# A hybrid attention block on one core: a host-transposed input normalised in place, sixteen gate steps at the front, and a tail two Strassen groups shorter

## The chip, the cores and the metric

The kernel runs on one core of a Trainium2 chip. The metric is the device time of one execution in microseconds; the kernel before takes 1904.11 (median of three runs, 1903.36 to 1904.30). A core has TensorE (PE in the profile), which multiplies matrices out of SBUF into PSUM; VectorE (DVE), ScalarE (ACT) and GpSimd (POOL), which work elementwise; and SyncE (SP), whose queue issues most of the DMA transfers here. Each engine works through its own list of instructions in order.

## The reference

One layer of a block over 2048 tokens of 1024 channels: an RMS norm, one wide projection for two attention mixers, SiLU gates on both mixers' outputs, and a sigmoid-weighted merge added to the residual. Cut to what matters here:

```python
h = rms_norm(x, norm_gain[layer])            # x * rsqrt(mean(x*x) + eps) * gain
proj = h @ w_in[layer]
qa, ka, va, qb, kb, vb, ga, gb, mg = jnp.split(proj, split_idx, axis=-1)
...                                          # banded attention A, dilated attention B
ya = ya.reshape(bsz, S, A_WIDTH) * jax.nn.silu(ga)     # ga: 512 channels
yb = yb.reshape(bsz, S, B_WIDTH) * jax.nn.silu(gb)     # gb: 512 channels
br_a = ya @ w_branch_a[layer]
br_b = yb @ w_branch_b[layer]
gates = jax.nn.sigmoid(mg...)
merged = gates[:, :, 0] * br_a + gates[:, :, 1] * br_b
x = x + merged @ w_out[layer]
```

The gates ga and gb are 1024 channels, so eight chunks of 128.

## The kernel before

**Numbers.** float32 products are made of float16 parts: each operand is split in a high and a low half, and a product is the sum of three matmuls (high by high, high by low, low by high) over eight chunks of 128 channels. One gate step is therefore 24 matmuls of 128x512. The normalised input lies in SBUF as XH and XL, channels on the partitions, tokens along the row.

**Stages.** (1) The input stage loads x, normalises it, makes XH and XL, and already computes two of the eight gate chunks. (2) The main stage projects and attends, unit by unit (unit A (0,0), A (1,0), then the dilated units), up to about 1230 us. In it, when a chunk of a mixer's output is ready for 512 tokens, a `YPart` transposes it on TensorE; for gate chunks 0 and 1 it fetches the stored gate, multiplies on VectorE (L966) and takes the maximum (L973), for the others ScalarE only copies it out (L964). (3) The tail computes the merge gates and the other six silu gate chunks with one level of Strassen's scheme: 19 groups in the order of the table `SEQ`, each 7 products of 12 matmuls (L1607). Entries 8, 9 and 10 of the table are the silu weights, two groups each, 1 to 7 the merge gates. Beside them the tail prepares the branch and output weights in 16 pieces, due between group 4 and group 17 (`K_AT`). (4) The branch products, the merge and the output projection follow.

**The input stage.** SP loads the gain (broadcast to all partitions, 512 KB), 16 tiles of x (128 tokens by 1024 channels, 512 KB each), two gate weights (512 KB) and four parts of the first unit's weights (384 KB). For each tile ScalarE squares and sums (L443), VectorE makes the inverse root with ScalarE's logarithm and exponential, and multiplies the tile by it and by the gain (L464); TensorE transposes it in eight pieces of 128x128 float32 (L484); ScalarE rounds the high half out of PSUM (L487) and VectorE subtracts for the low half (L491). As soon as 512 tokens are ready, two gate steps follow (L354), each with a tanh on ScalarE (L364), a gate product on VectorE (L371) and a store by SP (L377): four quarters by two chunks, eight steps.

**What sets the order.** In the input stage and in the tail a small planner does. Each step is entered with its engine, a cost in microseconds (`X_US` in the input stage), what it needs, and a rank; the planner plays the steps through these costs and writes them to the engines' lists in the order that comes out. On the chip only that order and the real dependences count. SP's loads stand in the order of `X_LD`.

## Time and profile before

| | |
|---|---|
| runs | 1903.36, 1904.11, 1904.30 us |
| profiled execution, span | 1902.2 us (from the first to the last instruction; the runs lie 1.2 to 2.1 above it) |
| granted TensorE clock | 1.000 |
| busy: TensorE, VectorE, ScalarE, GpSimd | 1871.2, 1499.1, 1249.0, 581.6 us |
| input stage ends (first main-stage matmul in the chain) | 80.90 us |
| Strassen groups, last before the standard steps | 1247.7 to 1580.5 us |

In the page, a group of instructions reads: line, engine, operation, output and inputs with their shapes and a count, then busy time, mean nanoseconds of one, the engine's idle time before it, and what ended that. A row of windows holds the stretch, then each engine's busy time with its number of instructions, then the granted clock, the DMA engines' mean share and GB/s. A row of the chain holds start, duration, engine and line of the piece that everything after waited for.

### The profile page before, as it was taken

What the parts mean: (1) busy time and instruction counts of PE and PEld (TensorE: products, weight loads), DVE (VectorE), ACT (ScalarE), POOL (GpSimd) and SP (SyncE); (2) the same over time, 40 slices, a digit from 0 to 9 for tenths busy, and PEclk for the clock granted to TensorE, in tenths of its full rate; (3) what the DMA queues carried; (4) which work ended last, traced back from release to release, by engine and by line L of the source; (5) the groups of instructions that cost most, each with busy time, mean ns of one, the idle gap of its engine ahead of it and who ended that gap; (6) DMA issues with size and microseconds to landing.
All of it is one profiled execution on the core that took longest, in us unless ns stands there. A gap on an engine that the chain in (4) does not pass through costs nothing.

```text
span 1902.2 us, 51103 instructions
## 1 busy us (share of the span) xinstructions
PE 1871.2 (98%) x19254; PEld 1439.5 (76%) x19254; DVE 1499.1 (79%) x3837; ACT 1249.0 (66%) x3015; POOL 581.6 (31%) x1363
## 2 busy tenths in 40 slices
...
GB/s 257 83 103 203 168 194 137 199 168 157 171 148 180 140 155 202 146 166 176 142 176 145 146 153 134 172 300 184 202 201 187 191 154 274 295 162 121 143 149 76
DMA packets 638983, 326.21 MB, mean 171 GB/s; under 512 B 458768, under 2 KB 589712, under 8 KB 636304
## 3 DMA queue, kind: packets, MB, share of 16 engines
...
q10 hardware_dynamic: 144, 0.26, 0.0%
...
## 4 chain that ended last, share of the span: by engine, by line
PE 91%; DMA 5%; DVE 1%; ACT 1%; issue 1%; SPq 0%; POOL 0%; DVEq 0%; POOLq 0%
PE pj L693 43%; PE fps L1607 18%; PE fps L1927 8%; PE fps L2012 7%; PE s L846 5%; PE pv L895 4%; PE pj L354 2%; DMA pt<-p 2%; PE pj L306 2%; DMA kq<-spl 1%; PE fps L306 1%; PE pt L959 1%; DMA bigl<-sd 1%; DMA graw<-in_w_gate_dram 0%; PE s L484 0%
## 5 line engine op out<-in xcount | busy, mean ns | idle before, releaser
L693 PE MATMUL pj<-wl,XH 128*128 128x128 f16 (+2 forms) x2816 | 715.2, 268 | 0.0
L693 PE MATMUL pj<-wh,XL 128*128 128x128 f16 (+2 forms) x2816 | 711.6, 269 | 0.0
L693 PE MATMUL pj<-wh,XH 128*128 128x128 f16 (+2 forms) x2816 | 708.6, 268 | 0.0
L693 PEld LDWEIGHTS <-XH 128*128 128x128 f16 x5632 | 574.9, 112 | 54.1
L693 PEld LDWEIGHTS <-XL 128*128 128x128 f16 x2816 | 315.8, 112 | 23.8
L861 DVE CUSTOM_DVE_ANT_0 pr<-s,b,ubuf 128x256 f32<-128x256 f32 (+3 forms) x512 | 218.7, 464 | 39.1 <-PE s L846 36.1
L878 DVE SCALAR_TENSOR_TENSOR p<-pr,p 128x512 f16<-128x512 f32 (+2 forms) x256 | 195.9, 765 | 49.7 <-ACT p L874 48.4
L760 POOL TENSOR_TENSOR rw<-rw,g 128x128 f32<-128x128 f32 (+1 forms) x224 | 149.2, 686 | 198.8 <-DVE rw L753 177.8
L1937 POOL TENSOR_TENSOR g<-g,t 128x512 f32<-128x512 f32 x32 | 48.4, 1514 | 522.1 <-DVE t L1859 521.6
L1607 PEld LDWEIGHTS <-wh 128*128 128x128 f16 x1064 | 104.2, 99 | 123.4 <-issue 0.3
L711 ACT ACTIVATE rw<-pj 128x256 f32<-128x256 f32 (+1 forms) x224 | 87.4, 390 | 135.8 <-PE pj L693 135.3
L775 POOL COPY spl<-spl 128x256 f16<-128x256 f16 (+1 forms) x224 | 97.4, 464 | 241.8 <-DVE spl L770 241.8
L874 ACT ACTIVATE p<-pr 128x512 f16<-128x512 f32 (+2 forms) x256 | 157.6, 616 | 10.7 <-DMA pt<-p 6.3
L846 PE MATMUL s<-kq 128*128 128x128 f16 (+1 forms) x1984 | 151.1, 217 | 2.7 <-DMA kq<-spl 1.6
L1927 PE MATMUL fps<-y,bigh 128*128 128x128 f16 x1792 | 153.4, 219 | 0.0
L1927 PE MATMUL fps<-y,bigl 128*128 128x128 f16 x896 | 151.7, 219 | 0.0
L2012 PE MATMUL fps<-WO,mf 128*128 128x512 f16 x660 | 147.5, 379 | 0.0
L846 PEld LDWEIGHTS <-kq 128*128 128x128 f16 x2016 | 131.0, 98 | 18.9 <-issue 3.5
L1927 PEld LDWEIGHTS <-bigh 128*128 128x128 f16 x1792 | 139.0, 98 | 7.3
L895 PE MATMUL pv<-vt,pt 128*128 128x65 f16 (+1 forms) x2784 | 131.6, 193 | 5.7 <-DMA pt<-p 5.7
L895 PEld LDWEIGHTS <-pt 128*128 128x128 f16 x3024 | 119.5, 97 | 21.0 <-DMA pt<-p 8.1
L766 ACT ACTIVATE spl<-rw 128x512 f16<-128x512 f32 (+1 forms) x112 | 72.0, 643 | 79.3 <-POOL vt L722 67.4
...
## 6 DMA issues: line engine op xcount, KB each, us to landing
...
g<-mgd SPq DMA_DIRECT2D x64, 256.0 KB, 5.1
wraw<-in_w_mrg_dram SPq DMA_DIRECT2D x45, 256.0 KB, 4.3
mgd<-t SPq DMA_DIRECT2D x43, 256.0 KB, 2.8
zd<-z SPq DMA_DIRECT2D x128, 66.0 KB, 2.0
...
xt<-in_x_dram SPq DMA_DIRECT2D x16, 512.0 KB, 8.0
ytd<-yo SPq DMA_DIRECT2D x32, 256.0 KB, 3.3
```

Source lines behind the costliest of these rows:

```text
L693: out.append(lambda lhs=lhs, rhs=rhs, ch=ch, a=a, b=b, k=k: T.matmul(ps[:, a:b], lhsT=lhs[:, ch, :], rhs=rhs[:, ch, a:b], start=(k == 0), ...
L711: A.activation(self.rw[:, n * i:n * i + n], self.ps[i][:, :n], AF.Copy)
L760: G.tensor_tensor(q[:, i, :un.nq, :], q[:, i, :un.nq, :], g, OP.mult)
L775: G.tensor_copy(sp[:, i, nh:, :, :], sp[:, i, nq:nh, ::-1, :])
L846: T.matmul(self.sv[j][:, o:o + k1 - k0], lhsT=q[:, h, :], rhs=kt[:, un.nq + kh + v * un.nk, k0:k1], start=(v == 0), stop=(v == 1))
L861: V.tensor_tensor_reduce(out=self.pv[:, j, self.p0:self.p0 + W], in0=self.sv[j], in1=un.bias[:, self.h0 + j, self.b0:self.b0 + W], scale=I ...
L874: A.activation(self.sp[:, :128 * n], self.pr, AF.Copy, scale=PSC)
L878: V.scalar_tensor_tensor(self.sp[:, 128 * n:], self.pr, PSC, self.sp[:, :128 * n], OP.mult, OP.subtract)
L895: T.matmul(self.po[:, j, :w], lhsT=p[:, n * j + s, :], rhs=un.v[key][:, vh, c0:c0 + w], start=(k == 0 and s == 0), stop=(k == 2 and s == n ...
L1607: T.matmul(b[k][:], lhsT=w[:, i, ch, :], rhs=xform(PROD[i][0], lo, ch, q), start=(i < 3 and n == 0), stop=(n == 11), skip_group_check=True)
L1927: out.append(lambda p=p, c=c, wl=wl, yl=yl, n=n: T.matmul(ps[:, 128 * p:128 * p + 128], lhsT=w[wl][:, i, c, p, :], rhs=y[:, yl, c, :], sta ...
L2012: out.append(lambda p=p, ml=ml, wl=wl, k=k: T.matmul(ps[:], lhsT=m[:, ml, p, :], rhs=WO[:, i, wl, p, :], start=(fresh and k == 0), stop=(k ...
```

## The change

**Input.** The host hands the kernel a second copy of x, transposed to eight chunks of 128 channels by 2048 tokens. It is loaded in five parts (256, 256, 512, 512 and 512 tokens) and normalised where it lies; there are no transposes. Parts 0 and 1 get their row sums from TensorE: a product of each 128 tokens with themselves (L525), whose diagonal VectorE sums (L512), and after the inverse root a diagonal matrix by ones (L565), which lays the factors along the row. Parts 2 to 4 still load tiles 4 to 15 of x as it was, for ScalarE's squares (L506); the inverse root is ten small operations on VectorE (L548 to L552), ScalarE's queue writes the four columns of 128 factors to memory (L572), and SP fetches them back as a row R, broadcast to all partitions (L576). The multiplication by R is VectorE's (L581) or GpSimd's (L583), by the table `X_DVE`; ScalarE makes the high half with the gain as its scale (L587), VectorE the low half from two operands in SBUF (L591).

**Gates.** Four chunks instead of two (`NSI`), so 16 steps (matmuls L383, tanh L393, product L400, store L406), the first quarter's in two halves of 256 tokens. The weights' norms are taken by TensorE (L329); chunks 2 and 3 are scaled and split on GpSimd (L373, L366). `YPart` takes the fetching and multiplying way for chunks 2 and 3 too, which come with unit A (1,0). Fourteen small matmuls stand ahead of everything on TensorE (L517).

**Tail.** `SEQ` loses the two groups of entry 10, so 17 groups, and the pieces' last due group is 15. `SX` and `VSC` are powers of two that scale numbers.

SP's queue, in which loads stand in the order in which they are issued (`xt` is the tile of x, `graw` a gate weight, `wraw` a unit's weight, `gtd` a stored gate). Before:

```order
L469 DMA gb<-in_gain_dram 128x1024
L423 DMA xt<-in_x_dram 128x1024 x4
L316 DMA graw<-in_w_gate_dram 128x1024
L423 DMA xt<-in_x_dram 128x1024 x2
L426 DMA qg<-in_qkg_dram 128x256
L427 DMA snk<-in_sink_dram 128x8
L428 DMA bmt<-in_b_merge_dram 128x16
L316 DMA graw<-in_w_gate_dram 128x1024
L423 DMA xt<-in_x_dram 128x1024 x8
L180 DMA wraw<-in_w_units_dram 128x768 x4
L423 DMA xt<-in_x_dram 128x1024 x2
```

Now, from the loads of tiles 4 to 7 on (ahead of them stand, in this order, the gain, two `xq`, two `graw`, two `xq`, the three small loads and two `graw`; `xq` is the transposed x, `rd` the factors in memory):

```order
L456 DMA xt<-in_x_dram 128x1024 x4
L464 DMA xq<-in_xt_dram 128x2x512 x4
L456 DMA xt<-in_x_dram 128x1024 x2
L183 DMA wraw<-in_w_units_dram 128x768 x4
L456 DMA xt<-in_x_dram 128x1024 x5
L576 DMA R<-rd 128x512
L464 DMA xq<-in_xt_dram 128x2x512 x4
L456 DMA xt<-in_x_dram 128x1024
L406 DMA gtd_88<-yo 128x512
L406 DMA gtd_89<-yo 128x512
L464 DMA xq<-in_xt_dram 128x2x512 x4
L576 DMA R<-rd 128x512
```

The first fetch of R stands behind 23 loads of 512 KB and four of 384 KB, where before all 16 tiles, the gain, both gate weights and the four `wraw` were 19 and four.

VectorE around the third quarter's tokens, before (a product with the factor, then low halves out of PSUM, `s`):

```order
L464 SCALAR_TENSOR_TENSOR xt<-xt,xr,gb 128x1024
L491 TENSOR_TENSOR XL<-s,XH 128x4x128 x3
L464 SCALAR_TENSOR_TENSOR xt<-xt,xr,gb 128x1024
L447 TENSOR_SCALAR xss<-xss 128x4
L491 TENSOR_TENSOR XL<-s,XH 128x4x128 x2
L371 SCALAR_TENSOR_TENSOR yo<-yo,pj 128x512
L491 TENSOR_TENSOR XL<-s,XH 128x4x128 x3
L371 SCALAR_TENSOR_TENSOR yo<-yo,pj 128x512
```

Now, the multiplications and low halves of parts 3 and 4:

```order
L581 TENSOR_TENSOR xq<-xq,R 128x512 x5
L400 SCALAR_TENSOR_TENSOR yo<-yo,pj 128x512
L591 SCALAR_TENSOR_TENSOR XL<-xq,gs,XH 128x512 x6
L400 SCALAR_TENSOR_TENSOR yo<-yo,pj 128x512
L591 SCALAR_TENSOR_TENSOR XL<-xq,gs,XH 128x512 x2
L581 TENSOR_TENSOR xq<-xq,R 128x512 x3
L400 SCALAR_TENSOR_TENSOR yo<-yo,pj 128x512
L591 SCALAR_TENSOR_TENSOR XL<-xq,gs,XH 128x512 x6
```

Every operation of VectorE between the gate products now has both operands in SBUF, where half of them had one in PSUM.

GpSimd, which had one copy in the stage before, now does this up to its first main-stage copy (L594):

```order
L583 TENSOR_TENSOR xq<-xq,R 128x256 x4
L373 TENSOR_SCALAR graw<-graw,gps_358 128x1024 x2
L366 TENSOR_TENSOR gl<-graw,gh 128x1024 x2
L583 TENSOR_TENSOR xq<-xq,R 128x256 x2
L583 TENSOR_TENSOR xq<-xq,R 128x512 x12
```

The twelve last rows' worth of products are those of parts 2, 3 and 4 that VectorE does not have.

The diff, cut to its core:

```diff
-VSC = 2.0 ** -16
-SX = 2.0 ** 8
+VSC = 2.0 ** -13
+SX = 2.0 ** 9
...
-SEQ = ((1, 0), (1, 1), (8, 0), (8, 1), (2, 0), (2, 1), (9, 0), (9, 1), (3, 0), (3, 1), (10, 0), (10, 1), (4, 0), (4, 1),
+SEQ = ((1, 0), (1, 1), (8, 0), (8, 1), (2, 0), (2, 1), (9, 0), (9, 1), (3, 0), (3, 1), (4, 0), (4, 1),
        (5, 0), (5, 1), (6, 0), (6, 1), (7, 0))
+NSI = 4
 G_T0, G_LD, G_SQ = 5.0, 6.0, 2.0
 W_RAW, L_LAST = 14.0, 0.4
-STD, W_EARLY, G_TH, G_SI, G_CP, K_AT = 5.2, 24.0, 2.0, 4.0, 1.0, (4, 17)
+STD, W_EARLY, G_TH, G_SI, G_CP, K_AT = 5.2, 24.0, 2.0, 4.0, 1.0, (4, 15)
 Y_S = 4.0
 Y_1 = (.2, .9, 1.6), (13.0, 14.0, 1.6)
 WO_AT = 2.0, 5.5
 M_AT = {0: (1.0, (5.0, 6.6, 8.2, 9.8, 11.4, 13.0, 14.6)), 1: (1.0, (6.5, 8.7, 10.9, 13.1, 15.3, 17.5, 19.7)),
         7: (.7, (3.5, 5.4, 7.3, 9.2, 11.1, 13.5, 26.4))}
-X_LD = ("g", 0, 1, 2, 3, "w0", 4, 5, "w1", 6, 7, 8, 9, 10, 11, 12, 13, "u")
-X_RK = (-35, 21, 20, -9)
-X_TR = 0.6
-X_NR = (-34, -92, 28)
-X_XR = (7, -126, 40, 10)
-X_GR = (29, 49)
-X_TWO = (0, 1, 2, 2)
-X_GF = (6.6, 15.2)
-X_TH = (45, 46, 85, 86, 125, 126, 165, 166)
+X_LD = ("g", "a0", "w0", "w1", "a1", "w2", "w3", 4, 5, 6, 7, "t2", 8, 9, 10, 11, "t3", 12, 13, 14, 15, "u", "t4")
+X_PART = ((0, 256), (256, 256), (512, 512), (1024, 512), (1536, 512))
...
+X_DVE = {0: ((), (0, 2, 4, 6)), 1: ((), (0, 1, 3, 4, 6, 7)), 2: ((), (0, 3, 5, 6)), 3: ((), (0, 3, 4, 5, 6)), 4: ((), (0, 2, 4))}
...
+XR_BUFS = 6
+XT_BUFS = 2
+X_WARM = 14
...
+    def g_gram(c, ch):
+        if ch == 0:
+            grams["g", c] = s_p.tile([128, 512], F32, name="s") if c % 2 else pj_p.tile([128, 512], F32, name="pj")
+        v = gw[c][0][:, ch, :]
+        T.matmul(grams["g", c][:, 0:128], lhsT=v, rhs=v, start=(ch == 0), stop=(ch == NCH - 1))
...
+    def g_lo(c, pool):
         gh, gl, ih, raw, s = gw[c]
-        V.scalar_tensor_tensor(gl[:], raw, s[:], gh[:], OP.mult, OP.subtract)
-        done.add(("g", c))
+        if pool:
+            G.tensor_tensor(gl[:], raw, gh[:], OP.subtract)
+        else:
+            V.scalar_tensor_tensor(gl[:], raw, s, gh[:], OP.mult, OP.subtract)
+    def g_scale(c):
+        gh, gl, ih, raw, s = gw[c]
+        gw[c] = (gh, gl, ih, raw, 1.0)
+        G.tensor_scalar(raw, raw, s, None, OP.mult)
...
-        ps = pj_p.tile([128, 512], F32, name="pj")
-        ts = slice(512 * q, 512 * q + 512)
-        out = []
-        for w, xx in ((gh, XH), (gh, XL), (gl, XH)):
-            for ch in range(NCH):
-                i = len(out)
-                out.append(lambda w=w, xx=xx, ch=ch, i=i: T.matmul(
-                    ps[:], lhsT=w[:, ch, :], rhs=xx[:, ch, ts], start=(i == 0), stop=(i == 23)))
-        return out, gate_steps(ps, c, q, ih, None)
+        ps = pv_p.tile([128, 512], F32, name="pv") if q == 0 and c > 1 else pj_p.tile([128, 512], F32, name="pj")
+        def mm(k, a, b):
+            w, xx = ((gh, XH), (gl, XH), (gh, XL))[k // NCH]
+            ch = k % NCH
+            T.matmul(ps[:, a:b], lhsT=w[:, ch, :], rhs=xx[:, ch, 512 * q + a:512 * q + b], start=(k == 0), stop=(k == 23))
+        return mm, gate_steps(ps, c, q, ih, None)
...
+    def t_load(p, i, n):
+        t0, m = X_PART[p]
+        if i == 0:
+            if p != 1:
+                xq[0] = sp0.tile([128, NCH, 512], F32, name="xq", bufs=XT_BUFS)
+            xtt[p] = xq[0][:, :, t0 % 512:t0 % 512 + m]
+        nc.sync.dma_start(out=xtt[p][:, i:i + n, :], in_=xt[i:i + n, :, t0:t0 + m].rearrange("c p t -> p c t"))
...
-    def x_scale(t):
-        i = t - groups[t][0]
-        V.scalar_tensor_tensor(xts[t][:], xts[t][:], xss[groups[t]][:, i:i + 1], gb[:], OP.mult, OP.mult)
...
-    def x_turn(t, h):
-        xps[t, h] = ps = s_p.tile([128, 4, 128], F32, name="s")
-        for c in range(4):
-            cc = 4 * h + c
-            T.transpose(ps[:, c, :], xts[t][:, 128 * cc:128 * cc + 128], idf[:])
-    def x_hi(t, h):
-        A.activation(XH[:, 4 * h:4 * h + 4, 128 * t:128 * t + 128], xps[t, h][:], AF.Copy)
-    def x_lo(t, h):
-        ts = slice(128 * t, 128 * t + 128)
-        V.tensor_tensor(XL[:, 4 * h:4 * h + 4, ts], xps[t, h][:], XH[:, 4 * h:4 * h + 4, ts], OP.subtract)
...
+    def x_warm(i):
+        if i == 0:
+            grams["w"] = pt_p.tile([128, 512], F32, name="pt")
+        T.matmul(grams["w"][:, 0:128], lhsT=ones[:], rhs=ones[:], start=True, stop=True)
+    def x_gram(p, c):
+        if c == 0:
+            for i in range(2):
+                grams[2 * p + i] = s_p.tile([128, 512], F32, name="s") if p == 0 else pv_p.tile([128, 512], F32, name="pv")
+        for i in range(2):
+            v = xtt[p][:, c, 128 * i:128 * i + 128]
+            T.matmul(grams[2 * p + i][:, 0:128], lhsT=v, rhs=v, start=(c == 0), stop=(c == NCH - 1))
+    def x_trace(t):
+        p, i = t // 2, t % 2
+        if i == 0:
+            rs_[p] = sp0.tile([128, 4], F32, name="xss", bufs=4)
+        trace(grams[t], rs_[p][:, i:i + 1])
...
+    def x_rsqrt(p):
+        ss = rs_[p][:]
+        y = sp0.tile([128, 4], F32, name="xy", bufs=4)
+        h = sp0.tile([128, 4], F32, name="xh", bufs=4)
+        V.tensor_scalar(y[:].bitcast(I32), ss.bitcast(I32), -0.5, float(0x5F3759DF), OP.mult, OP.add)
+        for k in range(3):
+            V.tensor_tensor(h[:], y[:], y[:], OP.mult)
+            V.scalar_tensor_tensor(h[:], h[:], -0.5, ss, OP.mult, OP.mult)
+            V.scalar_tensor_tensor(y[:] if k < 2 else ss, h[:], 1.5, y[:], OP.add, OP.mult)
+    dgs, rps = {}, {}
+    def x_diag(t):
+        p, i = t // 2, t % 2
+        dgs[t] = sp0.tile([128, 128], F32, name="dg", bufs=2)
+        V.tensor_scalar(dgs[t][:], idf[:], rs_[p][:, i:i + 1], None, OP.mult)
+    def x_row(t):
+        p, i = t // 2, t % 2
+        if i == 0:
+            rps[p] = s_p.tile([128, 512], F32, name="s")
+        T.matmul(rps[p][:, 128 * i:128 * i + 128], lhsT=ones[:], rhs=dgs[t][:], start=True, stop=True)
+    def x_rows(p):
+        Rt[p] = sp0.tile([128, 512], F32, name="R", bufs=2)
+        A.activation(Rt[p][:, 0:256], rps[p][:, 0:256], AF.Copy)
+    def x_spread(p):
+        nc.scalar.dma_start(out=rd[p - 2].rearrange("i t -> t i"), in_=rs_[p][:])
+    def x_fetch(p):
+        Rt[p] = sp0.tile([128, 512], F32, name="R", bufs=2)
+        nc.sync.dma_start(out=Rt[p][:], in_=rd[p - 2].rearrange("i t -> (i t)").unsqueeze(0).broadcast_to([128, 512]))
+    def x_mul(p, c, dve):
+        v = xtt[p][:, c, :]
+        if dve:
+            V.tensor_tensor(v, v, rps[p][:, 0:256] if p < 2 else Rt[p][:], OP.mult)
+        else:
+            G.tensor_tensor(v, v, Rt[p][:, :X_PART[p][1]], OP.mult)
+    def x_hi(p, c):
+        t0, m = X_PART[p]
+        A.activation(XH[:, c, t0:t0 + m], xtt[p][:, c, :], AF.Copy, scale=gs[:, c:c + 1])
+    def x_lo(p, c):
+        t0, m = X_PART[p]
+        V.scalar_tensor_tensor(XL[:, c, t0:t0 + m], xtt[p][:, c, :], gs[:, c:c + 1], XH[:, c, t0:t0 + m], OP.mult, OP.subtract)
...
+                elif p > 2:
+                    free = [("lo", b, c) for b in ((0, 1) if p == 3 else (2,)) for c in range(NCH)]
+            else:
+                f, args = x_load, (k,)
+                if k >= XR_BUFS + 4:
+                    free = [("sq", k - XR_BUFS)]
...
+            pool = c in X_GLP
+            if pool:
+                od.add(("gc", c), "G", us_["gc"], [("gp", a)], 0, g_scale, c)
+            od.add(("gh", c), "A", us_["gh"], [("gc", c) if pool else ("gp", a)], 0, g_hi, c)
+            od.add(("gl", c), *(("G", us_["pl"], [("gh", c)]) if pool else ("V", us_["gl"], [("gh", c)])), 0, g_lo, c, pool, first=X_GL1 if c == 1 else 0.0)
...
+    gates = [(q, c) for q in range(4) for c in range(NSI)]
+    runs = [(i, p) for p in range(2) for i in range(NSI)] + [(i, gates[i][0] + 1) for i in range(NSI, 4 * NSI)]
...
-            if self.chunk > 1:
+            if self.chunk >= NSI:
...
-        c = 2 + 2 * (dc - 8) + n
+        c = NSI + 2 * (dc - 8) + n
...
-        for c in range(8)] + [_rows(w[:, 5632 + 256 * c:5888 + 256 * c]) for c in range(3)])
+        for c in range(8)] + [_rows(w[:, 5376 + 256 * c:5632 + 256 * c]) for c in range(NSI // 2, 4)])
...
-    return [x[0], w_units, w_gate, w_mrg, wo, w_bra, w_brk, norm_gain, qkg, sink_a, bias_a, bias_b, bm]
-_INS = ["x", "w_units", "w_gate", "w_mrg", "w_out", "w_bra", "w_brk", "gain", "qkg", "sink", "bias_a", "bias_b", "b_merge"]
+    return [x[0], x[0].T.reshape(NCH, 128, S), w_units, w_gate, w_mrg, wo, w_bra, w_brk, norm_gain[0].reshape(NCH, 128).T, qkg, sink_a, bias_a, bias_b, bm]
```

326 lines of the change are left out of this document (209 added, 117 removed).

## The prediction

> **What bounds the kernel now.** I read the page's head first, then the core's windows, the chain of waits, and the groups. The head says which engine to watch:
>
> ```profile
> span 1902.2 us, 51103 instructions
> PE 1871.2 (98%) x19254; PEld 1439.5 (76%) x19254; DVE 1499.1 (79%) x3837; ACT 1249.0 (66%) x3015; POOL 581.6 (31%) x1363
> ```
>
> TensorE (PE) is busy for all but 31 us of the span. The stretches of ten microseconds show where most of those 31 us are; PE's busy time is the second number of a row.
>
> ```profile
> 0.00:10.00 10.00, 0.00 (x0) 0.00 (x0) 4.01 (x14) 4.72 (x8) 0.84 (x7) 1.00 0.80 299
> 10.00:20.00 10.00, 6.28 (x28) 5.77 (x28) 8.94 (x26) 9.20 (x22) 0.00 (x0) 1.00 0.98 376
> 20.00:30.00 10.00, 9.11 (x33) 4.55 (x34) 8.83 (x20) 9.90 (x19) 0.00 (x0) 1.00 1.03 418
> ...
> 60.00:70.00 10.00, 10.00 (x60) 6.03 (x60) 9.83 (x18) 7.46 (x11) 1.12 (x3) 1.00 0.09 33
> ...
> sum 90.00, PE 72.10 PEld 43.16 DVE 64.92 ACT 61.21 POOL 1.96; mean PE 8.01 PEld 4.80 DVE 7.21 ACT 6.80 POOL 0.22
> ```
>
> PE is idle for 17.9 of the first 90 us, 14.6 of them before 30 us, while DMA runs at 418 GB/s. So two prices count: loads until the first gate step, and PE time everywhere else. The chain gives both:
>
> ```profile
> 2.12 6.62 DMA xt<-in_x_dram
> 8.76 8.28 DMA graw<-in_w_gate_dram
> ...
> 22.83 7.79 PE pj L354 x27
> ...
> 68.16 0.87 PE s L484 x8
> 69.03 11.87 PE pj L354 x55
> 80.90 14.14 PE pj L693 x87
> ```
>
> The first gate matmul starts at 22.83, and the stage hands over to the main stage at 80.90. One warm gate matmul (L354) costs 11.87/55 = 0.2158 us, a step of 24 of them 5.18. One of the removed transposes (L484) costs 0.87/8 = 0.109.
>
> **The change, part by part.**
>
> *The tail.* Two of the 19 Strassen groups go, each 7 products of 4 chunks by 3 split terms = 84 matmuls (L1607).
>
> ```profile
> 1525.98 0.12 PE fps L191 x2
> 1526.10 54.41 PE fps L1607 x252
> 1400.00:1450.00 50.00, 50.00 (x234) 22.79 (x233) 38.91 (x81) 38.86 (x77) 0.00 (x0) 1.00 0.73 218
> 1500.00:1550.00 50.00, 50.00 (x235) 22.86 (x234) 35.50 (x76) 41.55 (x79) 0.00 (x0) 1.00 0.60 185
> ```
>
> One matmul is 54.41/252 = 0.2159, so two groups are 168 x 0.2159 = 36.3, plus one norm sum of 0.12 for the weight preparation that goes with them: **-36.4 us**. PE is busy for the whole of both windows, so nothing there now hides behind something else. The 16 weight pieces of the later table are now spread over 11 groups instead of 13. ACT's fullest window is 41.55 of 50; if nothing but the number of groups changed, that would be 41.55 x 13/11 = 49.1, just inside 50. The dropped gates' own work leaves too, so I charge nothing, and keep this as a rival.
>
> *The input stage, by PE's work.* 16 steps instead of 8 are 8 x 5.18 = +41.4; 128 transposes go, 128 x 0.109 = -14.0. That alone would move 80.9 to 108.3, if the waits stayed. The warm-up matmuls and the gram matmuls lie in PE's early idle time. But the waits are now others, so I also build the end from the loads.
>
> *When the second quarter can begin.* Parts 2 to 4 cannot be multiplied before R, the row of 512 token factors, has been fetched, and the first fetch stands on SP behind 23 loads of 512 KB, four of 384 KB and the small ones. SP's queue of before shows the pace, as each issue waits for an earlier load:
>
> ```profile
> 5.01 0.33 SPq L426 DMA_DIRECT2D qg<-in_qkg_dram  x1
> 6.27 0.33 SPq L427 DMA_DIRECT2D snk<-in_sink_dram  x1
> 7.52 0.33 SPq L428 DMA_DIRECT2D bmt<-in_b_merge_dram  x1
> 8.76 0.33 SPq L316 DMA_DIRECT2D graw<-in_w_gate_dram  x1
> ```
>
> So the first 512 KB land at 5.0 and then one each 1.25. The second graw, ninth of its size, should have landed at 5.0 + 8 x 1.25 = 15.0; by the chain it did at 8.76 + 8.28 = 17.04. The three small loads therefore cost 2.0. The 23rd lands at 5.0 + 22 x 1.25 + 2.0 = 34.5; four weight loads of three quarters size add 3.75, and R's 256 KB 0.6: **38.9**. R is read from a small write of r that comes from ACT's queue, and no write of such small elements is in this trace; the nearest rows are a store and the input loads:
>
> ```profile
> xt<-in_x_dram SPq DMA_DIRECT2D x16, 512.0 KB, 8.0
> ...
> gtd<-yo SPq DMA_DIRECT2D x1, 256.0 KB, 2.3
> ```
>
> Between 2.3 and 8.0 us from issue to landing, then, the long one for a write in the thick of the loads. The four squares that r needs belong to loads 9 to 12 (landed by 5.0 + 11 x 1.25 + 2.0 = 20.8) on an ACT that is busy for 9.90 of 10 us; with 6 us for its backlog r is written at 27 and lands at 29 to 35, ahead of its reader. If r is late, the fetch is.
>
> Work after R, by the nearest rows:
>
> ```profile
> L487 ACT ACTIVATE XH<-s 128x512 f16<-128x512 f32 x32 | 18.2, 595 | 6.3 <-PE s L484 5.9
> L443 ACT ACTIVATE jk<-xt 128x1024 f16<-128x1024 f32 x16 | 16.8, 1053 | 4.4 <-DMA xt<-in_x_dram 4.3
> L364 ACT ACTIVATE yo<-pj,ubuf 128x512 f32<-128x512 f32 x8 | 5.5, 688 | 11.1 <-PE pj L354 11.0
> L371 DVE SCALAR_TENSOR_TENSOR yo<-yo,pj 128x512 f32<-128x512 f32 x8 | 5.5, 681 | 9.7 <-ACT yo L364 9.7
> L272 DVE SCALAR_TENSOR_TENSOR rs_t<-rs_t,xss 128x4 f32<-128x4 f32 (+2 forms) x6 | 1.0, 162 | 0.2
> L1018 POOL TENSOR_TENSOR ya<-zz,am_e 128x512 f32<-128x512 f32 x14 | 19.6, 1399 | 6.1 <-DVE am_e L1013 4.8 <-PE s L846 0.9 <-PE pt L959 0.3
> L1491 DVE SCALAR_TENSOR_TENSOR wl<-wraw,ubuf,wh 128x512 f16<-128x512 f32 x32 | 23.6, 744 | 0.0
> ```
>
> In part 2 POOL multiplies four of the eight chunks, at 1.40 each: its fourth product is there at 38.9 + 5.6 = 44.5, its high half 0.6 later at 45.1, and then the step's last 17 matmuls take 3.7. The first step of quarter 2 ends at **48.8**. Eleven more steps are 57.0: **105.8**. Within a quarter (20.7 us) DVE has some 4 multiplies x 0.68, 8 low halves x 0.74, 4 gates x 0.68 and ten tiny steps of 0.16 for the next R: 13 us; ACT 8 x 0.6 + 4 squares x 1.05 + 4 tanh x 0.69: 11.8. Both fit, so quarters 3 and 4 follow without a gap, as PE did from 60 on. The reloads of x on SP wait for low halves of two quarters earlier at most, and R for quarter 3 is issued right behind four of them; at some 50 + 5 it is early for 64.
>
> Quarter 1 must not end after 48.8 - 5.2 = 43.6, so its 20.7 us of matmuls must begin by 22.9. Before's began at 22.83 with a tile's transposes and a broadcast gain in the way; now gram, norm, diagonal and row products stand there, but the first two loads suffice. I take it to fit, barely; each microsecond later is one on the end.
>
> *DVE beside POOL.* Before, POOL stood all but idle beside this stage (0.00 us in the rows of 10 to 30 above). Now it has 12 products of 128x512 in parts 2 to 4, next to a busy DVE. What that costs is seen late in before's trace:
>
> ```profile
> 1700.04 1.44 POOL L1937 TENSOR_TENSOR g<-g,t 128x512 f32<-128x512 f32 x1 [15.78 <-DVE t L1859]
> 1700.27 1.76 DVE L1972 SCALAR_TENSOR_TENSOR mf<-g,ubuf,mf 128x512 f16<-128x512 f32 x1
> L1972 DVE SCALAR_TENSOR_TENSOR mf<-g,ubuf,mf 128x512 f16<-128x512 f32 x49 | 47.3, 967 | 5.7 <-ACT mf L1968 5.7
> ```
>
> The same form of DVE operation takes 0.744 alone (L1491) and 1.76 when it meets a POOL product: 1.02 more. Over all 49 the excess is 0.967 - 0.744 = 0.22. The change's 36 DVE operations of parts 2 to 4 with two operands in SBUF (12 multiplies, 24 low halves) at 0.22 would be 7.9; DVE has 7 us spare in a quarter, so I take half on the path, **4.0**. The bounds are 0 and one full 1.02 for each of the 12 products, 12.2.
>
> The Trainium skill ("SBUF — State Buffer", section "SBUF: two separate sides") says that a DVE operation with two SBUF inputs and a GpSimd operation share a port pair under an exclusive lock, the loser blocking fully. The two rows of 1700 agree, 1.76 beside 1.44; by the rule every meeting costs in full, and the end would be the upper bound's, the first rival below.
>
> Input stage: 105.8 + 4.0 = 109.8, against 80.9: **+28.9**. Bounds: 106 to 118.
>
> *The main stage.* In unit (1,0), gate chunks 2 and 3 now fetch their stored gates (8 more loads of 256 KB) and multiply on DVE with a maximum after it, in place of a copy on ACT. Before has these for chunks 0 and 1, and PE's loss there:
>
> ```profile
> L966 DVE SCALAR_TENSOR_TENSOR yo<-pt,ubuf,yo x8: 733/741/747, 170.6 to 252.8; 128x512 f32<-128x512 f32 x8
> L973 DVE TENSOR_REDUCE ymx<-yo x8: 676/678/683, 172.3 to 254.3; 128x1 f32<-128x512 f32 x8
> 180.00:200.00 20.00, 17.65 (x302) 17.19 (x299) 16.96 (x42) 16.32 (x39) 6.87 (x18) 1.00 1.17 212
> 360.00:380.00 20.00, 19.12 (x240) 16.85 (x237) 18.29 (x44) 16.62 (x38) 9.07 (x17) 1.00 1.12 228
> ```
>
> That is 8 x (0.741 + 0.678) = 11.4 us more for DVE, which is already busy for 18.3 of 20 us there, and a gain of 8 copies for ACT. At 180 to 200 PE lost 2.4; at 360 to 380 it lost 0.9. Bounds 0 and 5 (twice 2.4, for 16 chunk steps instead of 8); I take **+2.5**.
>
> Sum: -36.4 + 28.9 + 2.5 = -5.0. The profiled execution spans 1902.2 us, its kernel's runs are 1903.36 to 1904.3, so some 1.2 to 2.1 lie around the span; from the median 1904.1 I get **1899.1 us**.
>
> **Rivals.**
>
> *R1, DVE and POOL exclude each other on the path.* Place: parts 2 to 4, multiplies and low halves that feed the next matmul; price 12.2 instead of 4.0, and about 2 in quarter 1, where POOL also scales and splits the weights of chunks 2 and 3 (four operations twice the size of L1018's, about 2.8 each). End 105.8 + 12.2 + 2 = 120.0, +39.1; total 1904.1 + 39.1 - 36.4 + 2.5 = **1909.3**. It decides from an end of 114.8 on (80.9 + 36.4 - 2.5), that is from 9 us of such waits. For it: 1.76 against 0.744. Against it: DVE's spare 7 us in a quarter, and the mean excess of only 0.22. An R that comes 9 us late, by its small write, would look the same in time.
>
> *R2, the main stage's DVE is full.* Unit (1,0) loses the bound's 5 instead of 2.5, and unit (0,0)'s stalls spread by as much again: **1904** or so, no change. For it: 18.29 of 20; against it: PE lost only 0.9 there.
>
> *R3, the tail saves less.* If ACT's 49.1 of 50 and the waits of the compressed pieces stop PE, a third of the 36.4 is lost: **1911**. Against it: DVE and ACT windows with 8 to 14 us free.
>
> *R4, nothing waits.* End at 105.8, no loss in the main stage: 1904.1 + 24.9 - 36.4 = **1892.6**.
>
> **How the numbers follow.** Forecast 0.50, R1 0.26, R2 0.10, R3 0.06, R4 0.08. A measurement of this kernel can tell about 0.2% (3.8 us) from no change, so faster means below 1900.3 and slower above 1907.9. The forecast's own range is 1895 to 1904: faster 0.38, same 0.12. R1 reaches from 1904 to 1911: slower 0.20, same 0.06. R2: same 0.08, slower 0.02. R3: same 0.03, slower 0.03. R4: faster 0.08. Sums: faster 0.46, same 0.29, slower 0.25. The range 1892 to 1910 leaves out the far ends of R3 and of R4.
>
> **What would show it.** Right: the first main-stage matmul near 110; the first R lands near 39; the tail's Strassen rows are 168 matmuls fewer with PE full between; quarters 3 and 4 without a gap in PE. R1: low halves and multiplies in the first 110 us with means well over 0.74, gaps in PE released by XL or XH. R2: gaps in PE at 350 to 460 released by DVE or by transposing DMAs. Wrong altogether: gram and norm work that starts quarter 1 after 23, or a squares queue on ACT that holds r back.

## The result and the profile after

The changed kernel takes 1945.57 us (median of four runs, 1943.92 to 1948.15) against 1904.07: a ratio of 1.0221, with a 95% interval of 1.0207 to 1.0236. It is 41.5 us slower, where 5 us faster was forecast. The page of its profiled execution begins:

```profile
span 1946.4 us, 51489 instructions
PE 1890.3 (97%) x19416; PEld 1455.8 (75%) x19416; DVE 1504.7 (77%) x3881; ACT 1233.3 (63%) x2978; POOL 615.0 (32%) x1385
```

TensorE is busy for 19 us more than before, but the span is 44 us longer: the other 25 are idle time. To see where, I cut both executions at three instructions: the first projection matmul of the main stage (L693, now L874), the first Strassen matmul (L1607, now L1789), the first branch product (L1927, now L2109).

| us | before | after | difference | forecast |
|---|---|---|---|---|
| input stage (start to first projection) | 80.7 | 148.6 | +67.9 | +28.9 |
| main stage (to the first Strassen matmul) | 1154.4 | 1164.2 | +9.8 | +2.5 |
| tail (to the first branch product) | 368.6 | 335.0 | -33.6 | -36.4 |
| rest | 298.5 | 298.6 | +0.1 | 0 |
| span | 1902.2 | 1946.4 | +44.2 | -5.0 |

The input stage by windows of ten microseconds (PE's busy time is the second number, then PE's weight loads, DVE, ACT, POOL; the last three numbers are the granted clock, DMA's share and GB/s):

```profile
20.00:30.00 10.00, 7.98 (x71) 6.86 (x70) 8.67 (x29) 7.47 (x15) 8.07 (x6) 1.00 1.04 395
30.00:40.00 10.00, 6.84 (x48) 4.97 (x47) 8.72 (x17) 5.14 (x11) 7.08 (x5) 0.89 0.80 302
40.00:50.00 10.00, 10.00 (x88) 8.68 (x87) 5.51 (x20) 8.68 (x16) 0.00 (x0) 0.94 0.71 16
50.00:60.00 10.00, 3.67 (x30) 2.71 (x28) 2.31 (x3) 1.21 (x3) 2.26 (x2) 0.91 0.83 213
60.00:70.00 10.00, 8.60 (x32) 3.43 (x32) 9.85 (x17) 8.75 (x15) 4.53 (x3) 0.74 0.44 167
...
80.00:90.00 10.00, 5.00 (x24) 2.14 (x22) 0.00 (x0) 0.00 (x0) 0.00 (x0) 0.95 0.93 212
90.00:100.00 10.00, 0.00 (x0) 0.00 (x0) 5.29 (x4) 3.85 (x6) 5.22 (x4) 0.50 0.48 81
100.00:110.00 10.00, 6.65 (x21) 2.40 (x21) 10.00 (x9) 5.80 (x9) 8.23 (x5) 0.70 0.08 28
```

From 53.1 to 57.7 and from 85.0 to 94.6 no engine computes, and TensorE itself stands until 59.2 and until 102.7. The chain of waits (pieces of the chain are left out at the dots) names what they all wait for:

```profile
42.07 8.97 DMA rd<-xss
51.12 6.55 DMA R<-rd
57.69 2.36 DVE xq L581 x2
...
63.40 4.99 DVE XL L591 x6
...
71.00 10.51 DMA rd<-xss
81.53 13.08 DMA R<-rd
...
102.68 7.43 DVE XL L591 x6
```

`rd<-xss` is the write of the 512 factors to memory, `R<-rd` the fetch of them as a row. Twice, for part 2 and for part 3, the factors make this trip through memory, in 15.6 and 23.6 us; TensorE still has matmuls for the first 11 and 14 us of them, and then stands. The trace puts the second wait of 17.7 us down to a gate product (L400), and that is right: the product ends at 102.68, and TensorE starts at 102.73. Its matmuls had been over since 79.8, but its tanh stands on ScalarE behind high halves of part 3 (at 97.79, where the first of them starts at 95.43), and the product itself on VectorE behind five multiplications by R (94.71 to 102.08). So it waited for the trip too, and for 8 us of work behind it.

And the operations themselves are slow. DVE's two groups of parts 2 to 4, with their mean time of one in nanoseconds, and, from the timeline, one small DVE operation beside two of POOL's:

```profile
L591 DVE SCALAR_TENSOR_TENSOR XL<-xq,gs,XH 128x512 f16<-128x512 f32 x24 | 20.9, 928 | 0.0
L581 DVE TENSOR_TENSOR xq<-xq,R 128x512 f32<-128x512 f32 x12 | 14.4, 1255 | 27.8 <-DMA R<-rd 27.8
```

```profile
31.26 4.41 POOL L366 TENSOR_TENSOR gl<-graw,gh 128x1024 f16<-128x1024 f32 x2
33.61 2.07 DVE L274 TENSOR_TENSOR rs_t<-rs_y 128x2 f32<-128x2 f32 x1
```

An operation on two columns takes 2.07 us, as it ends with POOL's at 35.67; the same form took 0.16 in the kernel before.

### The profile page after: what moved, and what is told of

Same layout as the page of the kernel before. It is cut to its first block, busy times and chain, and to the rows that moved or that the text cites. A ratio compares the mean times of both kernels' runs of the same rounds, so it can differ in the third digit from the quotient of the medians.

```text
span 1946.4 us, 51489 instructions
## 1 busy us (share of the span) xinstructions
PE 1890.3 (97%) x19416; PEld 1455.8 (75%) x19416; DVE 1504.7 (77%) x3881; ACT 1233.3 (63%) x2978; POOL 615.0 (32%) x1385
## 4 chain that ended last, share of the span: by engine, by line
PE 85%; DMA 6%; DVE 5%; issue 2%; POOL 1%; ACT 1%; SPq 0%; DVEq 0%; POOLq 0%; ACTq 0%
PE pj L874 40%; PE fps L1789 16%; PE fps L2109 8%; PE fps L2194 7%; PE s L1027 4%; PE pv L1076 4%; DMA pt<-p 2%; PE pj L383 2%; PE pj L310 2%; DMA kq<-spl 1%; PE fps L310 1%; DVE XL L591 1%; DMA R<-rd 1%; DMA rd<-xss 1%; DVE xq L581 1%
## 5 line engine op out<-in xcount | busy, mean ns | idle before, releaser
L874 PE MATMUL pj<-wl,XH 128*128 128x128 f16 (+2 forms) x2816 | 716.0, 268 | 0.0
L874 PE MATMUL pj<-wh,XL 128*128 128x128 f16 (+2 forms) x2816 | 712.4, 269 | 0.0
L874 PE MATMUL pj<-wh,XH 128*128 128x128 f16 (+2 forms) x2816 | 709.5, 268 | 1.1 <-DVE vt L910 1.1
L874 PEld LDWEIGHTS <-XH 128*128 128x128 f16 x5632 | 574.6, 112 | 56.1 <-issue 1.7
L874 PEld LDWEIGHTS <-XL 128*128 128x128 f16 x2816 | 315.4, 112 | 24.1 <-issue 0.3
L1789 PEld LDWEIGHTS <-wh 128*128 128x128 f16 x952 | 93.3, 99 | 113.3 <-issue 3.7
L2109 PE MATMUL fps<-y,bigh 128*128 128x128 f16 x1792 | 153.4, 219 | 0.0
L2109 PE MATMUL fps<-y,bigl 128*128 128x128 f16 x896 | 151.7, 219 | 0.0
L2109 PEld LDWEIGHTS <-bigh 128*128 128x128 f16 x1792 | 138.8, 98 | 7.3
```

The source lines that it names most:

```text
L874: out.append(lambda lhs=lhs, rhs=rhs, ch=ch, a=a, b=b, k=k: T.matmul(ps[:, a:b], lhsT=lhs[:, ch, :], rhs=rhs[:, ch, a:b], start=(k == 0), ...
L1789: T.matmul(b[k][:], lhsT=w[:, i, ch, :], rhs=xform(PROD[i][0], lo, ch, q), start=(i < 3 and n == 0), stop=(n == 11), skip_group_check=True)
L2109: out.append(lambda p=p, c=c, wl=wl, yl=yl, n=n: T.matmul(ps[:, 128 * p:128 * p + 128], lhsT=w[wl][:, i, c, p, :], rhs=y[:, yl, c, :], sta ...
```

## The experiments

Two theories stood after the two traces. **M**: the trip of the factors through memory sets the input stage's end, with the slow clock behind its gaps. **X**: DVE and POOL exclude each other, and that sets it. One thing to keep in mind with every edit of the input stage: the planner writes the engines' lists anew, so that other steps can move too.

### R by TensorE

```diff
...
-            od.add(("rw", p), "A", us_["rw"], [("nw", p)], 0, x_spread, p)
-            od.add(("rl", p), "D", us_["dma"], [("rw", p)], 0, lambda: None)
-            od.add(("rf", p), "S", .45, [("rl", p)], 0, x_fetch, p)
-            od.add(("re", p), "D", us_["dma"], [("rf", p)], 0, lambda: None)
+            for t in ts:
+                od.add(("dg", t), "V", us_["dg"], [("nw", p)], 0, x_diag, t)
+                od.add(("rb", t), "T", us_["rb"], [("dg", t)] + ([("rb", t - 1)] if t % 4 else []), 0, x_row, t)
+            od.add(("re", p), "A", .65, [("rb", ts[3])], 0, x_rows, p)
```

> The changed kernel, but for parts 2 to 4 the row R is made as for parts 0 and 1: a diagonal of the factors by ones on TensorE, copied by ScalarE. No write to memory, no fetch. Theory M (the trip of the factors through memory set the input stage's end: 42.07 to 57.67 for part 2 and 71.00 to 94.61 for part 3 in the changed kernel, and TensorE's granted clock fell to 0.50 and 0.74 in the gaps it left): R of part 2 is there some 2 us after its factors, 14 us earlier, part 3's 22 us earlier, and 2 to 5 us of slow clock go: the first main-stage matmul at 108 to 113 instead of 148.6, total 1903 to 1912. Theory X (VectorE and GpSimd exclude each other, and this sets the end): the exclusion stays, so that at most half of that comes back; first main-stage matmul at 125 or later, total 1923 or more.

Measured: 1919.88 us (1.0083, 1.0066 to 1.0101). The stage's first projection moves from 148.6 to 120.2, 28.4 us earlier; R of part 2 is copied at 46.8 instead of landing at 57.7. The chain now holds no DMA behind the first loads:

```profile
46.20 0.59 ACT R L570
...
94.32 26.06 PE pj L383 x120
120.38 14.62 PE pj L875 x90
```

So M holds for most of it, but 120.2 lies between what the two theories said, and 7 us above M's 108 to 113.

### No GpSimd in the input stage

```diff
-X_DVE = {0: ((), (0, 2, 4, 6)), 1: ((), (0, 1, 3, 4, 6, 7)), 2: ((), (0, 3, 5, 6)), 3: ((), (0, 3, 4, 5, 6)), 4: ((), (0, 2, 4))}
+X_DVE = {p: ((), tuple(range(8))) for p in range(5)}
-X_GB, X_GLP = ((0, 1), (1, 2), (2, 4)), (2, 3)
+X_GB, X_GLP = ((0, 1), (1, 2), (2, 4)), ()
```

> The changed kernel, but all multiplications by R and the preparation of gate weights 2 and 3 are VectorE's; GpSimd does nothing in the input stage. The trip of the factors through memory stays. Theory X: every meeting is gone, and with it the 1.45 us median of VectorE's multiplications (0.69 alone) and the two-microsecond small operations near 33 us: 15 us or more come back, total 1930 or less. Theory M: the two trips of 16 and 24 us stay on the path, and only some 3 us per part come back, total 1936 to 1946.

Measured: 1931.41 us (1.0143, 1.0118 to 1.0169, two runs), first projection at 132.5: 16 us earlier than in the changed kernel, although DVE now does all the multiplications. The total lies between the two ranges, nearer X's. The chain still holds two trips:

```profile
39.81 8.64 DMA rd<-xss
48.46 6.35 DMA R<-rd
...
88.34 10.79 DMA rd<-xss
99.14 4.38 DMA R<-rd
```

But the second of them is not part 3's any more. In the new lists part 3's factors stand ahead of part 2's multiplications. Here is the write of part 3's factors on ScalarE's queue, first in the changed kernel, then in this one:

```profile
71.00 0.37 ACTq L572 DMA_DIRECT2D rd<-xss  x1
```

```profile
45.03 0.37 ACTq L572 DMA_DIRECT2D rd<-xss  x1
```

So part 3's trip is hidden here, and the trip from 88.34 to 103.52 is part 4's. The 16 us are the exclusion and this change of order together, and the run does not separate them. The first trip is part 2's in both kernels: without GpSimd the factors are written at 39.81 instead of 42.07, and R lands 2.9 us earlier, though DVE does POOL's work as well. So both causes are real, and they stand in one chain: a blocked DVE delivers the factors late, and the trip comes on top.

### The factors of parts 3 and 4 earlier

```diff
-            mu=.73, pu=1.5, hi=.71, lo=.79, pw=1.3, gq=1.25, gh=1.15, gl=1.3, mm=.217, th=.69, gt=.66, us=1.03, uh=.94, ul=1.09, rw=.2, gc=1.6, pl=2.9, dma=2.3)
+            mu=.73, pu=1.5, hi=.71, lo=.79, pw=1.3, gq=1.25, gh=1.15, gl=1.3, mm=.217, th=.69, gt=.66, us=1.03, uh=.94, ul=1.09, rw=.2, gc=1.6, pl=2.9, dma=9.5)
```

> The changed kernel, but the planner is told that a trip takes 9.5 us each way instead of 2.3, so that it puts the factors of parts 3 and 4 on VectorE ahead of part 2's multiplications. Theory M, with the addition that the trips were serial only because part 3's factors stood behind part 2's low halves on VectorE (71.00, where the squares they need were done at 50): part 3's trip of 24 us is hidden behind part 2's matmuls, some 20 us come back, total 1920 to 1930. Theory X: the order changes nothing, 1940 or more.

Measured: 1949.00 us (1.0236, 1.0213 to 1.0259, two runs), a miss for M's addition. The trace shows why. The planner, told of long trips, also put other work ahead of the first fetch on SP's queue:

```profile
44.71 7.15 SPq L464 DMA_DIRECT2D xq<-in_xt_dram  x4
51.96 1.79 SPq L456 DMA_DIRECT2D xt<-in_x_dram  x1
53.85 2.12 SPq L406 DMA_DIRECT2D gtd<-yo  x2
56.92 9.41 SPq L576 DMA_DIRECT2D R<-rd  x2
```

The factors were written at 41.5, but their fetch was issued at 56.92, behind four loads of part 3, one of x and two gate stores, and R landed at 71.9. On VectorE the factors of part 4 and the first unit's weights then stood ahead of its share of part 2, which it began at 87.04. But for two small matmuls at 80.5, TensorE stood from 51.9 to 88.5. What then followed tells more than the total:

```profile
88.53 64.78 PE pj L383 x288
153.31 6.83 PE pj L874 x42
```

All 288 matmuls of quarters 2 to 4 ran in one piece of 64.8 us (288 x 0.2159 = 62.2). With the later rows fetched ahead, only the first trip is on the path. The edit moved the fetch and the weights too, so that it is no clean test of what earlier factors alone are worth.

### Fewer, larger packets for the write

```diff
-        nc.sync.dma_start(out=xts[t][:], in_=x[128 * t:128 * t + 128, :])
+        nc.sync.dma_start(out=xts[t][:], in_=x[512 * (t // 4):512 * (t // 4) + 512, :].rearrange("(k i) d -> i k d", i=4)[t % 4])
...
-    rd = dr.tile([3, 4, 128], F32, name="rd")
+    rd = dr.tile([3, 128, 4], F32, name="rd")
...
-        nc.scalar.dma_start(out=rd[p - 2].rearrange("i t -> t i"), in_=rs_[p][:])
+        nc.scalar.dma_start(out=rd[p - 2], in_=rs_[p][:])
```

> The changed kernel, but tile i of a part holds tokens 4k + i (k the partition) and not 128 neighbours, so that the four factors of a partition are neighbours in memory: the write is 128 pieces of 16 bytes and not 512 of 4. The order of the instructions is the same. If the write's 9 to 10.5 us are the price of its many packets: 2.5 to 4 us for a write, two trips on the path 6 to 7 us shorter each, total 1930 to 1936. If a write costs the same whatever its pieces: 1944 to 1948.

Measured: 1929.64 us (1.0134, 1.0117 to 1.0150), just below the forecast of 1930 to 1936: 15.9 us less than the changed kernel, for a change in the form of three writes of 2 KB. ScalarE's DMA queue (q10) and the writes' median time to landing (the last number), first of the changed kernel between 36 and 100 us, then of this one between 36 and 80:

```profile
q10 hardware_dynamic: 1584, 0.01, 1.3%
...
rd<-xss ACTq DMA_DIRECT2D x3, 2.0 KB, 10.5
```

```profile
q10 hardware_dynamic: 432, 0.01, 0.5%
...
rd<-xss ACTq DMA_DIRECT2D x3, 2.0 KB, 1.4
```

528 packets a write became 144, and the median of 10.5 us became 1.4, less than the 2.5 to 4 that were forecast (the three took 9.0, 10.5 and 20.2 in the changed kernel, and 1.4, 1.4 and 6.4 here). The Trainium skill ("DMA: Bandwidth & Descriptors", section "Rules for kernel authors") says that an access whose last dimension is strided goes as one descriptor per element, and to make it contiguous; the packet counts agree. The fetches, unchanged, are still long where they stand behind loads: 5.60 and 7.75 us. The first trip is 8.0 us (41.40 to 49.38) instead of 15.6, the second 11.1 (62.73 to 73.84) instead of 23.6: 20.1 together, and the stage's first projection, at 127.8, is 20.8 earlier.

### R by TensorE and no GpSimd

The diffs of the first two together.

> Both single edits together: R of every part by TensorE, and no multiplication or weight preparation on GpSimd in the input stage. Theory now: the trip through memory cost 28 us and the exclusion of VectorE by GpSimd the 11 us that were left over the forecast's 109.8 (the stage ended at 120.4 with R by TensorE). Then TensorE bounds the stage: 288 matmuls of 62.2 us behind the end of quarter 1 near 48, first main-stage matmul at 108 to 113, total 1904 to 1910. If VectorE is full without GpSimd's help, as it then has 8 multiplications a part: 118 or later, total 1915 or more.

Measured: 1919.22 us (1.0083, 1.0065 to 1.0101), first projection at 120.0: not a microsecond from the kernel that still had POOL's share (each of the two totals is known to some 3.4 us), and so a miss. DVE's operations did become as short as they are alone:

```profile
L592 DVE SCALAR_TENSOR_TENSOR XL<-xq,gs,XH 128x512 f16<-128x512 f32 x24 | 16.3, 745 | 0.0
L582 DVE TENSOR_TENSOR xq<-xq,R 128x512 f32<-128x512 f32 x24 | 15.1, 684 | 0.2 <-ACT R L570 0.2
```

0.684 instead of 1.255, and 0.745 instead of 0.928: exclusion cost the changed kernel 12 x 0.571 + 24 x 0.183 = 11.2 us of DVE's time in parts 2 to 4. But DVE was not what waited last. Of ScalarE's waits between 40 and 121 us:

```profile
ACT yo L393 <- DMA gtd<-yo: 7.9, 3, 5.6
```

A tanh writes into one of three tiles, and a tile is free once SP has stored the gate that was in it. Sixteen steps go through three tiles, and the store took 4 us from 64.05 and again from 69.61 in this kernel's chain. With POOL's share it was the same: 8.3 us, in three places.

### Five gate tiles, without and with GpSimd

The edit on the last kernel (two more tiles out of the stage's own pool; one tile of x fewer pays for them):

```diff
-            th.append(gp.tile([128, 512], F32, name="yo", bufs=3))
+            th.append(gp.tile([128, 512], F32, name="yo", bufs=3) if m is not None or (NSI * q + c) % 5 < 3 else
+                      sp0.tile([128, 512], F32, name="yg", bufs=2))
-XR_BUFS = 6
+XR_BUFS = 5
```

> As the kernel with R by TensorE and no GpSimd, with five tiles for a gate's tanh instead of three (and five of x instead of six, for the room). That kernel's stage ended at 120.0, with quarter 1 over at 52 and 62.2 us of matmuls behind it; ScalarE's tanh waited 7.9 us in three places for the store of a gate to free its tile. If that ring holds the stage: the first main-stage matmul at 114 to 116 and 3 to 6 us less than that kernel, total 1913 to 1916. If VectorE holds it: within 1.5 us of it.

The same with GpSimd's share as in the changed kernel:

> As the run beside it with five gate tiles, but with GpSimd's share of the multiplications and weights given back (R by TensorE stays). With R by TensorE and three gate tiles, GpSimd's share made no difference in time (1919.9 with it, 1919.2 without), although it had cost 14 us where R came through memory. If three tiles hid it: 4 us or more above the run beside it. If with R early the exclusion lies beside TensorE's work: within 2 us of it.

Measured: 1913.80 us (1.0060, 1.0045 to 1.0075) without POOL, first projection at 116.7, and no wait of ScalarE for a store any more; 1920.14 us (1.0095, 1.0072 to 1.0117) with POOL, first projection at 121.7. The four runs of the one (1913.12 to 1916.65) and of the other (1917.09 to 1926.56) do not overlap. So the ring of three tiles had hidden the exclusion, and with the ring out of the way exclusion costs 5.0 us of the stage, 6.3 of the total. With POOL five tiles gain nothing: there VectorE's multiplications and low halves make up most of the chain from 48 to 95. The stage in all six kernels:

| first projection, us | R through memory | R by TensorE, 3 gate tiles | R by TensorE, 5 gate tiles |
|---|---|---|---|
| GpSimd shares the work | 148.6 | 120.2 | 121.7 |
| VectorE alone | 132.5 | 120.0 | 116.7 |

The rows differ by 16, 0 and 5 us. The 5 I put down to the exclusion (VectorE's lists differ there too, as it has more to do without GpSimd), the 0 to the ring, and the 16 hold the changed order of part 3's factors as well.

### The tail alone

On the kernel before:

```diff
-SEQ = ((1, 0), (1, 1), (8, 0), (8, 1), (2, 0), (2, 1), (9, 0), (9, 1), (3, 0), (3, 1), (10, 0), (10, 1), (4, 0), (4, 1),
+SEQ = ((1, 0), (1, 1), (8, 0), (8, 1), (2, 0), (2, 1), (9, 0), (9, 1), (3, 0), (3, 1), (4, 0), (4, 1),
-STD, W_EARLY, G_TH, G_SI, G_CP, K_AT = 5.2, 24.0, 2.0, 4.0, 1.0, (4, 17)
+STD, W_EARLY, G_TH, G_SI, G_CP, K_AT = 5.2, 24.0, 2.0, 4.0, 1.0, (4, 15)
...
```

> The kernel before with the tail's edit alone: the two groups of entry 10 leave the table, the pieces' last due group is 15; nothing takes up their work, so gate chunks 6 and 7 are left out. If the tail's saving is real: 36.4 less than before, total 1866 to 1870. If the compressed weight pieces hold TensorE up (the third rival of the prediction): a third is lost, total 1876 or more.

Measured: 1867.76 us, 36.3 less than the 1904.06 beside it. TensorE stays full in every window of 50 us from 1250 to 1550.

### The main stage: what of the gate work costs

Three kernels touch the outputs for gate chunks 2 and 3. The first is the changed kernel with the old way for them:

```diff
-            if self.chunk >= NSI:
+            if self.chunk >= 2:
                 A.activation(self.o[:], self.ps[:], AF.Copy)
```

(and the same bound where the gate is fetched and where the maximum is taken).

> The changed kernel, but in the main stage the outputs for gate chunks 2 and 3 are only copied by ScalarE, as before: their gates are computed and stored and never applied, so that part of the result is left out. In the changed kernel TensorE loses 6.6 us more than before between 280 and 360 us after the main stage begins, the place of these chunks, and the main stage is some 9 us longer. If their fetch, product and maximum are the cause: total 1936 (1934 to 1939). If the loss has another cause (a shifted order of SP's transposing transfers): 1943 or more.

Measured: 1940.82 us, a miss by 2 us; the main stage is 1157.3, 6.9 shorter than the changed kernel's, but this execution's input stage was 1.5 us longer.

The second is the kernel with R by TensorE and no GpSimd, with another queue for the fetches:

```diff
-            nc.sync.dma_start(out=self.o[:], in_=gtd[self.chunk]...
+            (nc.scalar if self.chunk > 1 else nc.sync).dma_start(out=self.o[:], in_=gtd[self.chunk]...
```

> As the kernel with R by TensorE and no GpSimd, and the eight fetches of stored gates of chunks 2 and 3 are issued from ScalarE's queue and not from SP's. If they cost by standing ahead of the transposing transfers of the attention weights on SP (2.08 us for one fetch's issue at 425 in the changed kernel, with a wait of TensorE for such a transfer right behind it): 4 to 7 us less than the kernel without this edit. If they cost by VectorE's 11.4 us of work there: within 1.5 us of it.

Measured: 1921.35 us against 1919.22, main stage 1166.0 in both: the order on SP's queue is not it.

The third starts from the kernel with five gate tiles:

```diff
+            if self.chunk > 1:
+                c = gp.tile([128, 512], F32, name="yo", bufs=3)
+                A.activation(c[:], self.ps[:], AF.Copy, scale=gw[self.chunk][2])
+                G.tensor_tensor(self.o[:], self.o[:], c[:], OP.mult)
+                return
             V.scalar_tensor_tensor(self.o[:], self.ps[:], gw[self.chunk][2], self.o[:],
                                    OP.mult, OP.mult)
```

> As the kernel with five gate tiles and no GpSimd in the input stage, and in the main stage the products of gate chunks 2 and 3 are taken from VectorE: ScalarE copies the transposed output with the scale, GpSimd multiplies by the gate, VectorE keeps the maximum. The main stage is 9 to 12 us longer than before's 1154.4 in all kernels with this part of the change; without these products at all it was 1157.3. If VectorE's eight products (5.9 us on an engine busy for 18.3 of 20 us there) are the cause: 3 to 6 us less than the run with five gate tiles. If GpSimd's eight products shut VectorE out instead, or if the fetches are the cause: within 1.5 us or slower.

Measured: 1917.10 us against 1913.80, main stage 1164.1 against 1162.9: taking the products from VectorE and giving them to GpSimd does not help either. This does not clear VectorE's products: the expectation's last case, that GpSimd's do as much harm, gives the same.

So a fourth kept the fetches alone, from the same kernel: the copy overwrites the fetched gate, and no maximum is taken.

> The kernel with five gate tiles, R by TensorE and no GpSimd in the input stage; in the main stage the stored gates of chunks 2 and 3 are still fetched, but ScalarE overwrites them with the plain copy: the product with the gate and the maximum are left out. The main stage was 1154.4 us before, 1157.3 without any of the three (fetch, product, maximum), 1162.9 in the kernel with five gate tiles; moving the fetches to ScalarE's queue or the products to GpSimd changed it by no more than 1.2 to the better. If VectorE's product, maximum and scales are the cause: 1157 to 1159 and a total some 5 us lower, 1907 to 1910. If the fetches are the cause: 1162 or more, total 1912 to 1916.

Measured: 1912.71 us against 1913.80, main stage 1160.4 against 1162.9: between the two theories. The windows show that there are two places. These are 40 us each, beginning 280 and 320 us after the first projection; before first, then the kernel with the old way, the one with fetches alone, the one with five gate tiles:

```profile
360.70:400.70 40.00, 39.12 (x494) 34.87 (x493) 35.82 (x97) 35.01 (x86) 16.85 (x34) 1.00 1.02 194
400.70:440.70 40.00, 40.00 (x345) 35.33 (x344) 33.19 (x91) 29.90 (x86) 19.15 (x47) 1.00 0.71 165
```

```profile
430.10:470.10 40.00, 38.45 (x491) 34.27 (x490) 35.34 (x94) 33.45 (x84) 17.15 (x34) 1.00 1.05 192
470.10:510.10 40.00, 39.67 (x342) 34.87 (x340) 32.66 (x90) 30.09 (x86) 18.60 (x47) 1.00 0.73 163
```

```profile
397.10:437.10 40.00, 35.19 (x438) 30.77 (x437) 32.47 (x83) 31.41 (x77) 14.56 (x31) 1.00 1.11 196
437.10:477.10 40.00, 40.00 (x345) 35.12 (x344) 33.29 (x96) 30.05 (x89) 19.08 (x45) 1.00 0.92 178
```

```profile
396.70:436.70 40.00, 36.20 (x460) 31.80 (x459) 36.97 (x91) 31.60 (x76) 16.62 (x34) 1.00 1.06 206
436.70:476.70 40.00, 37.83 (x315) 32.62 (x314) 36.03 (x104) 25.02 (x74) 16.11 (x38) 1.00 0.88 169
```

In the first stretch TensorE loses 0.9, 1.6, 4.8 and 3.8 us: the fetches alone bring the whole loss. (DMA's share is over 1 in all four.) With fetches alone, TensorE's waits around it are for the transposed attention weights:

```profile
PE pv L1078 <- DMA pt<-p: 4.8, 4, 2.5
```

In the second it loses 0, 0.3, 0 and 2.2: that is VectorE's product, maximum and scales. Each place is worth 2 to 4 us in these executions. The other kernels bear it out: in all eight that fetch and multiply as the changed kernel does, TensorE loses 3.5 to 4.8 us in the first stretch and 2.0 to 2.7 in the second. In the changed kernel a wait from 438.3 to 441.1, in the first stretch, also took the granted clock (third from last) down to half for 3.4 us:

```profile
440.00:450.00 10.00, 8.94 (x106) 7.46 (x107) 5.68 (x14) 7.16 (x16) 0.99 (x3) 0.83 1.02 190
```

That is another 1.7 us, an estimate from half of those 3.4. That the fetches slow the transposing transfers on the DMA engines themselves, and not in a queue, fits the second kernel's null result but was not measured by itself.

## Why the prediction was wrong

**When the second quarter can begin: the step that failed.** It put the factors' write at 27, its landing at 29 to 35, and R at 38.9, 0.6 us behind the last load. The order was read rightly (23 loads stand ahead of the fetch), but the fetch waited for the factors, not for the loads. The factors were written at 42.07, as the squares they need ended at 34.6 on ScalarE and VectorE then still had part 1's norm and multiplications in front of them, held up by POOL; the write took 9.0 where 2.3 to 8.0 was allowed for; the fetch took 6.55 where 0.6 was. R came at 57.7, 18.8 us late. The text said that no write of such small elements was in the trace, and then treated its price as hidden, since its end was thought to come before a reader that was itself misplaced. The table from which it took its bounds held a nearer row than the input loads, a small transfer among them, and it lies above the bound of 8.0:

```profile
snk<-in_sink_dram SPq DMA_DIRECT2D x1, 4.0 KB, 9.6
```

"If r is late, the fetch is" was there; no case had its price.

**"Quarters 3 and 4 follow without a gap."** Wrong by more. R for quarter 3 was to be early, at 55 for 64. On VectorE its factors stand behind part 2's low halves, which wait for part 2's R, so the trips are in series: written at 71.00, fetched by 94.61, and TensorE idle from 85.0 to 102.7. The last 8 us of that gap came after R, as a gate product that TensorE needed stood behind five multiplications by R. The list of VectorE's rows in which this can be read had been looked at for its load only, not for what the next R stands behind. The run with R by TensorE gives the size of both steps together, with the lists as the planner then wrote them: 28.4 us of the stage.

**Quarter 1.** It had to begin by 22.9 and end by 43.6. It began at 21.3, but ended at 53.1: its 20.7 us of matmuls took 31.8. TensorE was idle for 5.2 us between 20 and 40 for high and low halves, part 1's factors and weights, its clock was below full in two windows (0.89 and 0.94), and the gram products of weight 3 (1.8 us) stand inside the quarter. The text took it "to fit, barely"; it was 9.5 us late. In the changed kernel this stayed hidden behind R, which came 4.6 us later still. With everything else mended (five tiles, VectorE alone) it shows: there quarter 1 ends at 49.4, quarters 2 to 4 run from 50.6 to 116.7, for 62.2 us of matmuls, and the forecast's end was 109.8.

**VectorE beside POOL.** The mean of 0.22 per operation and half of it on the path gave 4.0, with 12.2 as the bound. VectorE's excess was 11.2 in parts 2 to 4 alone, the bound's size, and the stage lost 5 us to it with R early and enough tiles. With R through memory its part of the 16 us is not known. The mean of 0.22 came from a stage where POOL was busy for a quarter of the time; here POOL runs whole bursts beside a chain that cannot get out of its way. The Trainium skill's rule of an exclusive lock ("SBUF — State Buffer", section "SBUF: two separate sides") described this better than the mean: the 128x2 operation of 2.07 us that ends with POOL's operation agrees with it, and a low half of 0.745 alone became 0.928 on average.

**The first rival** had the right mechanism and an end of 120.0 for the stage. The changed kernel ended at 148.6, as that rival priced no trip; its sentence that a late R "would look the same in time" named the other cause. The two added up, which no case allowed for. That the kernel with R by TensorE ends at 120.2 does not confirm the rival's 120.0: without GpSimd's share that kernel ended at 120.0 as well, held by the gate tiles.

**The tail.** -36.4 was right: -36.3 by itself. Inside the changed kernel it is -33.6 between the two marks: the Strassen groups start with a wait for `bigh` and `bigl`, an operand that DMA brings, and behind that wait, which was some 1.5 us longer than before, the granted clock was at half from 1321.2 to 1324.6. The rival that weight pieces stop TensorE is out.

**The main stage.** +2.5 with bounds of 0 and 5; +9.8 in the changed kernel, of which 6.9 go when the gates of chunks 2 and 3 are not applied. The term counted VectorE's 11.4 us, and took PE's loss at the same work in unit (0,0). It named the eight fetches but gave them no price of their own, and by the last run they are the larger part; nor did it have the half clock behind a wait, by that estimate 1.7 us of the 9.8. The remaining 2.9 were not traced to a part of the change. The main stage differed by up to 5 us between kernels that are the same there (1162.4 to 1167.3), in part by the clock too: it was full throughout the shortest, and at half twice, for 3.4 us each, in the longest.

**The sum.** None of the kernels that compute everything beats the one before. The nearest is 1913.80, 10.7 us slower than the 1903.07 beside it; in its profiled execution (span 1911.4, 9.2 more than before) the stage's +36.0 and the main stage's +8.5 stand against -35.5 in the tail.
